# Dilated attention stage: weight, merge and staging transfers issued from ScalarE's queue, and half of a merge one step later

## The chip, the cores and the metric

One core of a Trainium2 chip. The metric is device time in microseconds (us) from start to end of one execution; lower is better. Engines: PE (TensorE), DVE (VectorE), ACT (ScalarE), POOL (GpSimd), and SP (SyncE), which only issues transfers (DMAs).

## What is computed

A bidirectional encoder of two layers on 1024 tokens of width 1024 in float32. Layer 0 mixes tokens by latent attention, layer 1 by dilated sliding-window attention; each layer ends with a squared-ReLU MLP. The change is in layer 1's mixer:

```python
DIL_GROUPS = ((128, 1), (512, 4), (2048, 16))     # (window, dilation)
def dilated_mixer(h, pos, w_in, g_q, g_k, rel_bias, w_o):
    proj = (h @ w_in).reshape(B, S, N_DIL_GROUPS, 3, DIL_HEADS, DIL_HEAD_DIM)
    for gi, (window, dilation) in enumerate(DIL_GROUPS):
        q = rms_norm(proj[:, :, gi, 0], g_q[gi])
        k = rms_norm(proj[:, :, gi, 1], g_k[gi])
        v = proj[:, :, gi, 2]
        o, lse = dilated_group(q, k, v, pos, table, window, dilation)
    wts = jax.nn.softmax(jnp.stack(lses, axis=0), axis=0)
    o = jnp.einsum('gbsh,gbshd->bshd', wts.astype(o_all.dtype), o_all)
    return o.reshape(B, S, DIL_HEADS * DIL_HEAD_DIM) @ w_o
```

So there are three groups of 16 heads of width 64, with a relative-position bias, and for every token the three groups' outputs are merged with weights from their softmax denominators.

## The kernel before

The stage is the method `dil()`. It runs over a list of steps: three groups, in each eight pairs of heads (`pr`), in each pair four steps (`tp`) of a quarter of the tokens. Between groups stands a step without projection (`None`), in which the normalized input is permuted for the next dilation (casts into `hTp`, L2097 and L2099). A step takes some 9 us.

One step works on three things at once. PE computes the scores of an earlier step (`pss`, L1869), the query and key projections of this step (`psproj`, L414 to L416, each product in three float32 pieces of a high and a low part), transposes of the queries and keys of the step before (`psq`, L1844), and the product of probabilities and values (`psav`, L1937 and L1938).

The chain of a step, off PE: DVE adds the bias tile `bt` and takes the maximum (`pd`, L1883), ACT negates it (`dnb`, L1887), exponentiates (L1889) and writes the high half of the probabilities (`ph`, L1923), POOL or DVE the low half (L1924). SP then issues a transposing DMA (`pT`, L1925), and psav reads pT. Alongside, ACT squares the projection (`dsq`, L1828), DVE sums it (`dms`, L1829), ACT takes a logarithm and an exponential (`drl`, `dry`, L112 and L113), DVE and POOL scale (`qn`, L1833 and L1835), PE transposes (psq), and ACT and DVE write the key tile in two parts (`kT`, L1848 and L1849), which the next step's pss reads.

The transfers of the stage, all from SP's queue:

- `wqkr`: the weights of the pair two steps ahead, four DMAs for each pair (`dil_weights`, L1551, called by `fetch`). ACT makes the high part (`wqkh`, L121), DVE the low one (`wqkl`, L122).
- `bt`: two bias tiles for each step (L1878). `vraw`: values (L1788 to L1804).
- `U`: the outputs of groups 1 and 2, written to memory (L1955, L1959). `um`: these outputs read back for the merge in group 3, four DMAs for each pair (L2041). `oTd`: merged and transposed outputs of pairs 0 to 5, written to memory (L2032).
- `pT`: the transposes (L1925), one for each step.

The merge is in group 3: `finish` (L1949) runs when a pair's attention is done. `factors` (L1982) turns the stored maxima and sums into weights with small operations (L1992 to L1998); `merge` multiplies and adds (L2007, L2009), five operations of 128x512 on DVE for each half of the tokens. Before, both halves follow at once; in the next step `emit` transposes them on PE and stores them (`oTd`).

The order on each engine is not the order of the code. A scheduler places the instructions of all engines, and each engine then runs its own list strictly in order. An instruction whose semaphore isn't there holds everything behind it on its engine. Each DMA of SP's queue, and of ACT's, takes one of eight completion lanes (DMAHW0 to DMAHW7) in turn, and waits for the DMA that had the lane before to land.

Of the kernel before, what the change touches and what calls it, by code (L numbers as in the profile page):

```python
# [41 lines left out]
class K:  # L42
# [1496 lines left out]
        v = dram.rearrange("(l r) d -> r l d", r=16)  # L1539
        return [(64 * i, 64, v[2 * t + i]) for i in range(2)]  # L1540

    def dil_weights(self, g, pr, alloc=None):


        w_in = self.a["dil_w_in"][0]
        raws = []
        for half in range(2):
            raw = (alloc or self.G)("wqkr", (P, 4, 256), F32)
            for k in range(2):
                c0 = (g * 3 + k) * 1024 + 2 * pr * 64  # L1550
                self.nc.sync.dma_start(out=raw[:, :, k * P : (k + 1) * P],  # L1551
                                       in_=w_in[half * 512 : (half + 1) * 512, c0 : c0 + P].rearrange("(d p) f -> p d f", p=P))
            raws.append(raw)

        def split():
            out = []
            for raw in raws:
                hi, lo = self.G("wqkh", (P, 4, 256)), self.G("wqkl", (P, 4, 256))
                self.split(hi, lo, raw)
                out.append((hi, lo))  # L1560
            return out

        return split
# [185 lines left out]
    def dil(self, at0, at1, tail, wqk, vd):  # L1749
# [194 lines left out]
                last(u, 0)  # L1944

        O = [[[None] * 4 for _ in range(2)] for _ in range(2)]
        merged = []

        def finish(u):  # L1949
            g, pr = u["g"], u["pr"]  # L1950
            U = u["U"]
            if g < 2:
                dst = Ud[pr, :, g, :]
                if g == 0:
                    nc.sync.dma_start(out=dst.rearrange("(t p) e -> p t e", p=P), in_=U)  # L1955
                else:
                    v = dst.rearrange("(l p r) e -> p r l e", r=4, p=P)
                    for l in range(2):
                        nc.sync.dma_start(out=v[:, :, l, :], in_=U[:, l::2, :])  # L1959
                if pr == 7:  # L1960
                    sv = stat[:, g].rearrange("p t k h -> p t (k h)")
                    if g == 0:
                        nc.sync.dma_start(out=Sd[g].rearrange("(t p) e -> p t e", p=P), in_=sv)
                    else:
                        v = Sd[g].rearrange("(l p r) e -> p r l e", r=4, p=P)
                        for l in range(2):
                            nc.sync.dma_start(out=v[:, :, l, :], in_=sv[:, l::2, :])
                return

            if pr == 0:  # L1970
                for k in range(2):
                    v = Sd[k].rearrange("(l t r) e -> r l t e", t=8, r=2)
                    for i in range(2):
                        nc.sync.dma_start(out=stat[64 * i : 64 * i + 64, k].rearrange("p t k h -> p t (k h)"), in_=v[i])
            if pr < 7:
                f = factors(pr, 0, 8)
                for hf in range(2):
                    merge(u, hf, f[:, :, 4 * hf : 4 * hf + 4])
                merged.append((u, u["at"], (0, 1)))
            else:  # L1980
                last(u, 1)

# [33 lines left out]
        def emit(u, ths):  # L2016

            pr = u["pr"]
            if pr == 6:
                for k in range(2):  # L2020
                    for th in range(2):
                        O[k][th][3] = self.G(f"oT{k}", (P, 2, 512))
            for th in ths:
                ps = PS("psot")
                for i in range(4):
                    nc.tensor.transpose(ps[:, i * P : (i + 1) * P], u["U"][:, 4 * th + i, :], self.ident)
                if pr >= 6:
                    self.split(O[0][th][3][:, pr - 6, :], O[1][th][3][:, pr - 6, :], ps)
                else:
                    s_ = self.G("oT", (P, 2, 512))  # L2030
                    self.split(s_[:, 0, :], s_[:, 1, :], ps)
                    nc.sync.dma_start(out=oTd[pr, th], in_=s_.bitcast(F32))  # L2032

        def um(u, hfs):

            u.setdefault("um", [])
            v = Ud[u["pr"]].rearrange("(l t r) k e -> r l t (k e)", t=8, r=2)
            for hf in hfs:
                x = self.G("um", (P, 4, 2, P), F32)
                for i in range(2):  # L2040
                    nc.sync.dma_start(out=x[64 * i : 64 * i + 64].rearrange("p t k e -> p t (k e)"), in_=v[i][:, 4 * hf : 4 * hf + 4, :])  # L2041
                u["um"].append(x)


# [8 lines left out]

        def fetch(n):
            if n in firsts:
                loads[n] = self.dil_weights(*firsts[n][1:3])

        def fetch_split(n):
            if n in firsts:
# [51 lines left out]
        for n, step in enumerate(steps):  # L2111
# [23 lines left out]
            for u_, t_, _ in scored:  # L2135
                if u_["g"] == 2:
                    if u_["pr"] < 7:
                        if t_ == 7:
                            um(u_, (0, 1))
                    elif t_ in (1, 5):  # L2140
                        um(u_, (t_ // 4,))
            if step is not None:
                ps = PS("psproj")
                project(h, w, ps, 0, 2 * tp)
# [204 lines left out]
```

## Time and profile before

| | us |
|---|---|
| median of three runs | 3288.84 (3288.83 to 3289.92) |
| the profiled execution | 3296.57 |
| span of its trace | 3294.7 |
| dilated stage in the trace | 1645 to 2620 |
| PE busy, whole span | 3150.8 (96%) |
| DVE, ACT, POOL busy, whole span | 2406.2, 1735.6, 878.1 |

PE is the engine that works nearly all of the time, so an idle microsecond of PE is the thing to look for. The page's strip of 40 slices shows PE at nine tenths nearly everywhere; the stage lies in slices 20 to 32, where its clock is at nine tenths too, with 0.70 and 0.83 in the windows of the two changes of group (1950 to 1990 and 2260 to 2300). The busy shares of the other engines are averages over stages with different limits, and don't say which of them PE waits for; the waits do. A wait is put down to the semaphore that came last.

### The profile page before, as it was taken

The page shows a single profiled execution, that of the slowest core. Times are in us where ns is not written, and L with a number is a line of the kernel's source. Part 1 is how long each engine was busy: PE and PEld are TensorE (multiplying, and loading weights), DVE is VectorE, ACT ScalarE, POOL GpSimd, SP SyncE. Part 2 cuts the span into 40 slices and gives each one's busy share as a digit, 9 for nine tenths or more (in the row PEclk, how much of TensorE's full clock was granted, in tenths as well). Part 3 has the DMA queues.
Part 4 walks back from the last instruction along what each step waited for, and adds up shares of the span by engine and source line. Part 5 has one row for each costly group of instructions (what it writes and reads, how often), then busy time and mean ns, then how long its engine had stood idle before and what let it go on. Part 6 is the DMA issues. An engine that isn't in the chain of part 4 may idle for free. (4 is left out here: it accounts for less than half of the span.)

```text
span 3294.7 us, 50852 instructions
## 1 busy us (share of the span) xinstructions
PE 3150.8 (96%) x18034; PEld 2660.6 (81%) x18034; DVE 2406.2 (73%) x4272; ACT 1735.6 (53%) x3507; POOL 878.1 (27%) x1197
## 2 busy tenths in 40 slices
PE   6989999999999999899999979998998999999999
PEld 6877677778888788778899979997988788888887
DVE  5677777757977866787667776777778678778566
ACT  5547787755544433542246665667555355444342
POOL 7455555520111000001134343444333001110010
PEclk9999999999999999999999989998999999999999
DMA  5352322152654788536558866777777735439554
GB/s 189 119 186 82 103 94 88 63 191 78 213 185 170 279 243 283 168 106 209 195 142 177 189 149 161 180 169 161 146 174 169 211 96 204 143 143 322 205 191 128
DMA packets 538990, 552.31 MB, mean 168 GB/s; under 512 B 199493, under 2 KB 421106, under 8 KB 538730
## 3 DMA queue, kind: packets, MB, share of 16 engines
q1 hardware_dynamic: 511370, 457.69, 49.2%
q0 software_dynamic: 27360, 91.31, 7.5%
q8 instruction: 144, 2.36, 0.3%
q14 instruction: 116, 0.95, 0.1%
HBM read 376.17 MB, written 132.62 MB: 154 GB/s over the span
## 5 line engine op out<-in xcount | busy, mean ns | idle before, releaser
L415 PE MATMUL psm<-dl,dh 128*128 128x512 f32 x896 | 351.1, 392 | 8.5 <-DVE dl L122 8.4
L414 PE MATMUL psm<-hf,wf 128*128 128x512 f32 x896 | 350.1, 391 | 2.6 <-ACT wf L121 2.6
L416 PE MATMUL psm<-dh,dl 128*128 128x512 f32 x896 | 350.1, 391 | 0.0
L415 PE MATMUL psm<-hf,wf 128*128 128x512 f32 x896 | 349.6, 390 | 0.0
L416 PE MATMUL psm<-hf,wf 128*128 128x512 f32 x896 | 346.9, 390 | 0.4 <-DVE wf L122 0.4
L414 PE MATMUL psm<-dh,dh 128*128 128x512 f32 x896 | 335.0, 391 | 4.8 <-ACT dh L121 4.8
L414 PE MATMUL psproj<-wqkh,hTp 128*128 128x256 f32 x1024 | 306.0, 299 | 0.0
L415 PE MATMUL psproj<-wqkl,hTp 128*128 128x256 f32 x1024 | 293.9, 287 | 0.0
L416 PE MATMUL psproj<-wqkh,hTp 128*128 128x256 f32 x1024 | 293.5, 287 | 0.0
L121 ACT ACTIVATE dh<-ufr 128x1024 fp32r<-128x1024 f32 x112 | 118.3, 1057 | 175.8 <-PE psm L416 51.0
L414 PEld LDWEIGHTS psproj<-wqkh,hTp 128*128 128x128 f32 x1024 | 200.5, 196 | 9.2 <-issue 1.6
L415 PEld LDWEIGHTS psm<-dl,dh 128*128 128x128 f32 x896 | 169.0, 189 | 46.3 <-DVE dl L122 11.6
L414 PEld LDWEIGHTS psm<-dh,dh 128*128 128x128 f32 x896 | 168.3, 188 | 42.1 <-ACT dh L121 7.3
L414 PEld LDWEIGHTS psm<-hf,wf 128*128 128x128 f32 x896 | 168.6, 188 | 40.2 <-ACT wf L121 5.5
L415 PEld LDWEIGHTS psproj<-wqkl,hTp 128*128 128x128 f32 x1024 | 200.7, 196 | 0.0
L416 PEld LDWEIGHTS psproj<-wqkh,hTp 128*128 128x128 f32 x1024 | 200.3, 196 | 0.0
L416 PEld LDWEIGHTS psm<-hf,wf 128*128 128x128 f32 x896 | 168.5, 188 | 36.1 <-DVE wf L122 1.2
L416 PEld LDWEIGHTS psm<-dh,dl 128*128 128x128 f32 x896 | 169.0, 189 | 35.2
L415 PEld LDWEIGHTS psm<-hf,wf 128*128 128x128 f32 x896 | 168.6, 188 | 34.6
L122 DVE TENSOR_TENSOR dl<-ufr,dh 128x1024 fp32r<-128x1024 f32 x112 | 136.8, 1222 | 78.1 <-ACT dh L121 59.5
L745 DVE TENSOR_REDUCE mx<-pmx 128x1 f32<-128x512 f32 x256 | 165.2, 682 | 28.2 <-PE pmx L743 27.9
L1924 POOL TENSOR_TENSOR ph<-pd,ph 128x512 f16<-128x512 f32 (+1 forms) x120 | 122.8, 1028 | 226.9 <-ACT ph L1923 211.4
(399 smaller groups left out, 8950.1 us busy)
## 6 DMA issues: line engine op xcount, KB each, us to landing
ufr<-uf SPq DMA_DIRECT2D x112, 512.0 KB
adaw<-in_ada_w SPq DMA_DIRECT2D x96, 512.0 KB
w2r<-in_mlp_w SPq DMA_DIRECT2D x96, 512.0 KB
w1r<-in_mlp_w SPq DMA_DIRECT2D x64, 512.0 KB
bt<-bias SPq DMA_DIRECT2D x128, 256.0 KB
wqkr<-in_dil_w_in SPq DMA_DIRECT2D x96, 256.0 KB
qkv<-st SPq DMA_DIRECT2D x32, 512.0 KB
hraw<-qkv SPq DMA_DIRECT2D x32, 512.0 KB
```

Of the source, the lines that this page charges most:

```text
L121: nc.scalar.activation(hi, src, AF.Copy)
L122: (lo_eng or nc.vector).tensor_tensor(lo, src, hi.bitcast(F32), op=ALU.subtract)
L414: mm(out, lh, rh, start=first, stop=False)
L415: mm(out, lh, rl, start=False, stop=False)
L416: mm(out, ll, rh, start=False, stop=last)
L745: nc.vector.tensor_reduce(maxes[h][:, 2 * j + b : 2 * j + b + 1], ps, op=ALU.max, axis=AX.X)
L1924: (nc.gpsimd if i or g == 2 else nc.vector).tensor_tensor(lo, p, hi, op=ALU.subtract)
```

## The change

Three kinds of transfer are issued by `nc.scalar` (ACT's queue) instead of `nc.sync` (SP's): `wqkr` as called by `fetch` (92 of 96; the first pair's four stay with SP), all 32 `um`, all 12 `oTd`: 136 DMAs. The sizes and the addresses are the same. In group 3, `finish` merges only the first half of the tokens, with factors for that half; the second half, with its own factors, is put on the list `merging` and done in the next step, ahead of the projections, and is emitted a step later than before. That adds six small DVE operations and one exponential for each of seven pairs.

```diff
-    def dil_weights(self, g, pr, alloc=None):
+    def dil_weights(self, g, pr, alloc=None, eng=None):
...
-                self.nc.sync.dma_start(out=raw[:, :, k * P : (k + 1) * P],
+                (eng or self.nc.sync).dma_start(out=raw[:, :, k * P : (k + 1) * P],
...
-        merged = []
+        merged, merging = [], []
...
             if pr < 7:
-                f = factors(pr, 0, 8)
-                for hf in range(2):
-                    merge(u, hf, f[:, :, 4 * hf : 4 * hf + 4])
-                merged.append((u, u["at"], (0, 1)))
+                merge(u, 0, factors(pr, 0, 4))
+                merged.append((u, u["at"], (0,)))
+                merging.append((u, 1))
             else:
                 last(u, 1)
...
-            if pr == 6:
+            if pr == 6 and 0 in ths:
...
-                    nc.sync.dma_start(out=oTd[pr, th], in_=s_.bitcast(F32))
+                    nc.scalar.dma_start(out=oTd[pr, th], in_=s_.bitcast(F32))
...
-                    nc.sync.dma_start(out=x[64 * i : 64 * i + 64].rearrange("p t k e -> p t (k e)"), in_=v[i][:, 4 * hf : 4 * hf + 4, :])
+                    nc.scalar.dma_start(out=x[64 * i : 64 * i + 64].rearrange("p t k e -> p t (k e)"), in_=v[i][:, 4 * hf : 4 * hf + 4, :])
...
-                loads[n] = self.dil_weights(*firsts[n][1:3])
+                loads[n] = self.dil_weights(*firsts[n][1:3], eng=nc.scalar)
...
+            if merging:
+                u_, hf = merging.pop(0)
+                merge(u_, hf, factors(u_["pr"], 4 * hf, 4))
+                merged.append((u_, n, (hf,)))
             if step is not None:
                 ps = PS("psproj")
                 project(h, w, ps, 0, 2 * tp)
```

Since the scheduler places all of it anew, the order changes in more places than these. Three of them follow. The numbers in the names tell buffers apart; what an instruction waits for stands in brackets.

**ACT in group 3, the step in which a pair's weights and `um` are loaded.** Before, from the step's squares (`dsq`) to `kT`:

```order
L1828 ACTIVATE dsq_31206<-psproj_31138 128x512 [waits PE_49,Pool_49]
L121 ACTIVATE wqkh_31359<-wqkr_31224 128x1024 [waits DMAHW1_49,DMAHW0_49,DVE_49]
L112 ACTIVATE drl_31211<-dms_31207,eps 128x8 [waits DVE_49]
L113 ACTIVATE dry_31210<-drl_31211 128x8 [waits Activation_49]
L1887 ACTIVATE dnb_31248<-stat,ln_20890 128x2 [waits DVE_49]
L1887 ACTIVATE dnb_31259<-stat,ln_20890 128x2 [waits DVE_49]
L1889 ACTIVATE pd_31245,stat<-pd_31245,dnb_31248 128x128 [waits Activation_49]
L1889 ACTIVATE pd_31245,stat<-pd_31245,dnb_31248 128x128
L1889 ACTIVATE pd_31256,stat<-pd_31256,dnb_31259 128x128 [waits Activation_49,Pool_49]
L1889 ACTIVATE pd_31256,stat<-pd_31256,dnb_31259 128x128
L1923 ACTIVATE ph_31241<-pd_31245 128x256 [waits DMAHW3_49,Activation_49]
L1848 ACTIVATE kT_30951<-psq_31297 128x2x256 [waits PE_49]
```

The changed kernel, the first part of the same step:

```order
L1828 ACTIVATE dsq_31217<-psproj_31140 128x512 [waits PE_49,Pool_49]
L121 ACTIVATE oT_31201<-psot_31196 128x512 [waits PE_49]
L1551 DMA wqkr_31232<-in_dil_w_in 128x4x128 [waits DMAHW7_49]
L1551 DMA wqkr_31232<-in_dil_w_in 128x4x128 [waits DMAHW1_49]
L112 ACTIVATE drl_31222<-dms_31218,eps 128x8 [waits DVE_49]
L1551 DMA wqkr_31235<-in_dil_w_in 128x4x128 [waits DMAHW2_49]
L113 ACTIVATE dry_31221<-drl_31222 128x8 [waits Activation_49]
L1551 DMA wqkr_31235<-in_dil_w_in 128x4x128 [waits DMAHW3_49]
L2031 DMA oTd<-oT_31201 128x1024 [waits DMAHW4_49,DVE_49]
L1887 ACTIVATE dnb_31259<-stat,ln_20890 128x2 [waits DVE_49]
```

and its second part:

```order
L2040 DMA um_31277<-U 64x4x256 [waits DMAHW6_49]
L1889 ACTIVATE pd_31256,stat<-pd_31256,dnb_31259 128x128 [waits Activation_49]
L1889 ACTIVATE pd_31256,stat<-pd_31256,dnb_31259 128x128
L1887 ACTIVATE dnb_31270<-stat,ln_20890 128x2 [waits DVE_49]
L2040 DMA um_31277<-U 64x4x256 [waits DMAHW0_49]
L1923 ACTIVATE ph_31252<-pd_31256 128x256 [waits Activation_49]
L1889 ACTIVATE pd_31267,stat<-pd_31267,dnb_31270 128x128 [waits Activation_49,Pool_49]
L1889 ACTIVATE pd_31267,stat<-pd_31267,dnb_31270 128x128
L2040 DMA um_31280<-U 64x4x256 [waits DMAHW1_49]
L2040 DMA um_31280<-U 64x4x256 [waits DMAHW2_49]
L1923 ACTIVATE ph_31252<-pd_31267 128x256 [waits Activation_49]
L1848 ACTIVATE kT_30946<-psq_31308 128x2x256 [waits PE_49]
```

Nine DMAs now stand among the step's activations. Four `um` lie between `dnb` and the second `ph`; the third and the fourth wait for the lanes of the second and third `wqkr` (DMAHW1 and DMAHW2). `kT` comes behind the second `ph`, where it stood ahead of it, and the split of the weights (`wqkh`) has left the place behind `dsq`.

**SP at the change from group 1 to group 2.** Before:

```order
L1925 DMA_TRANSPOSE pT_24870<-ph_24869 128x16x128 [waits DVE_49,DMAHW0_49,PE_49,Pool_49]
L1878 ISA
L1878 DMA bt_25218<-bias_135 128x2x256 [waits DMAHW5_49,DMAHW1_49,DVE_49]
L1878 ISA
L1878 DMA bt_25282<-bias_135 128x2x256 [waits DMAHW6_49,DMAHW2_49,DVE_49]
L1878 ISA
L1878 DMA bt_25293<-bias_135 128x2x256 [waits DMAHW7_49,DMAHW3_49,DVE_49]
L1878 ISA
L1878 DMA bt_25418<-bias_135 128x2x256 [waits DMAHW4_49,DMAHW1_49,DVE_49]
L1925 DMA_TRANSPOSE pT_25024<-ph_25023 128x16x128 [waits PE_49,Pool_49]
```

The changed kernel:

```order
L1925 DMA_TRANSPOSE pT_24870<-ph_24869 128x16x128 [waits DVE_49,DMAHW0_49,PE_49,Pool_49]
L1878 ISA
L1878 DMA bt_25218<-bias_135 128x2x256 [waits DMAHW4_49,DMAHW1_49,DVE_49]
L1878 ISA
L1878 DMA bt_25282<-bias_135 128x2x256 [waits DMAHW6_49,DMAHW2_49,DVE_49]
L1925 DMA_TRANSPOSE pT_25024<-ph_25023 128x16x128 [waits DVE_49,DMAHW5_49,PE_49,Pool_49]
L1878 ISA
L1878 DMA bt_25293<-bias_135 128x2x256 [waits DMAHW7_49,DVE_49]
L1878 ISA
L1878 DMA bt_25418<-bias_135 128x2x256 [waits DMAHW1_49,DVE_49]
```

Two bias loads that wait for DVE have moved behind the transpose `pT_25024`. On POOL, the low half `ph_25023` that it needs has moved ahead of two casts into `hTp`.

**SP at the change from group 2 to group 3.** Before:

```order
L1878 DMA bt_29893<-bias_136 128x2x256 [waits DMAHW5_49,DMAHW1_49,DVE_49]
L1925 DMA_TRANSPOSE pT_29608<-ph_29607 128x16x128 [waits DMAHW0_49,DVE_49,DMAHW6_49,PE_49,Pool_49]
L1959 DMA U<-U_28598 512x1x128 [waits DVE_49]
L1878 ISA
L1878 DMA bt_29905<-bias_136 128x2x256 [waits DMAHW2_49,DVE_49]
```

The changed kernel:

```order
L1878 DMA bt_29893<-bias_136 128x2x256 [waits DMAHW5_49,DMAHW1_49,DVE_49]
L1959 DMA U<-U_28598 512x1x128 [waits DVE_49]
L1925 DMA_TRANSPOSE pT_29608<-ph_29607 128x16x128 [waits DMAHW0_49,DMAHW7_49,PE_49,Pool_49]
L1878 ISA
L1878 DMA bt_29905<-bias_136 128x2x256 [waits DMAHW2_49,DVE_49]
```

The store of `U_28598`, which waits for DVE's reduction of `psav`, has moved ahead of the transpose.

## Prediction

> **What bounds the kernel now.** I read the page first, then the windows of the dilated stage, then what TensorE (PE) waits for there, by group, and last the timelines around the longest of those waits. A window row holds its length and the busy time of PE, PE's weight loads, DVE, ACT and POOL, then the granted clock, the DMA share and GB/s; the first is group 3 with its pair steps, the second the sum of six windows from 1645 to 2620 us. A wait row holds total us, times, longest.
>
> ```profile
> 2300.00:2560.00 260.00, 240.14 (x2105) 227.91 (x2104) 206.61 (x595) 145.86 (x499) 87.06 (x108) 0.96 0.73 163
> sum 975.00, PE 905.47 PEld 847.96 DVE 715.08 ACT 575.02 POOL 349.70; mean PE 150.91 PEld 141.33 DVE 119.18 ACT 95.84 POOL 58.28
> PE psav L1937 <- DMA pT<-ph: 40.4, 22, 11.3
> PE pss L1869 <- DVE kT L1849: 16.0, 14, 6.1
> ```
>
> The change touches only this stage, and there PE is busy for 905.5 of 975 us. So 69.5 us, 2.1% of the span, is all that any rearrangement could win, and 40.4 of them are spent in front of the probability products psav, until the transposed probabilities pT have landed. The second cause, 16.0, is the key tile kT in front of the scores pss. The same question for pT asked in the windows of group 1 (1645 to 1950), group 2 (1990 to 2259) and group 3 (2300 to 2560) gives these rows, the fourth being kT in group 3:
>
> ```profile
> PE psav L1937 <- DMA pT<-ph: 8.1, 8, 2.1
> ...
> PE psav L1937 <- DMA pT<-ph: 3.5, 5, 1.7
> ...
> PE psav L1937 <- DMA pT<-ph: 16.2, 6, 4.5
> PE pss L1869 <- DVE kT L1849: 1.9, 3, 0.8
> ```
>
> The rest of pT's 40.4, 12.6, lies at the two changes of group (1950 to 1990, 2259 to 2300). Whether SyncE's queue (SP) is to blame differs: SP's own waits say whom the transpose stood waiting for, in group 1 and in group 3.
>
> ```profile
> SPq L1925 <- DVE ph L1924: 32.1, 16, 4.1
> ...
> SPq L1925 <- POOL ph L1924: 43.7, 17, 5.0
> ```
>
> In group 1 DVE's ph alone held 16 of the transposes (others waited for POOL): SP was free before the data was there, so taking work off SP helps little. In group 3 it is 17 of about 30 (one in each step of some 9 us); the others found SP occupied or had been delayed otherwise. One pair's turn shows how:
>
> ```profile
> 2347.25 1.43 SPq L1551 DMA_DIRECT2D wqkr<-in_dil_w_in  x2
> ...
> 2349.45 1.70 SPq L1551 DMA_DIRECT2D wqkr<-in_dil_w_in  x2
> ...
> 2352.24 3.40 SPq L2041 DMA_DIRECT2D um<-U  x4
> ...
> 2357.28 3.40 SPq L1925 DMA_TRANSPOSE pT<-ph  x1
> ...
> 2352.83 0.67 POOL L1924 TENSOR_TENSOR ph<-pd,ph 128x256 f16<-128x256 f32 x1
> ...
> 2364.31 0.34 PE L1937 MATMUL psav<-vs,pT 128*128 128x192 bf16 x1 [4.32 <-DMA pT<-ph]
> ```
>
> ph was complete at 2353.50, the transpose was issued at 2357.28, 3.8 us late, because two weight loads and four um loads went first; it then took 7.0 us to land, and PE stood 4.32 us.
>
> **The change, part by part.** What moves is issue time. The three rows give min, median and maximum in ns on SP.
>
> ```profile
> L1551 SPq DMA_DIRECT2D wqkr<-in_dil_w_in x96: 368/536/1582, 1614.8 to 2498.2; - x96
> ...
> L2041 SPq DMA_DIRECT2D um<-U x32: 579/615/1419, 2313.6 to 2568.3; - x32
> ...
> L2032 SPq DMA_DIRECT2D oTd<-oT x12: 502/590/1180, 2346.6 to 2533.1; - x12
> ```
>
> 92 x 0.536 + 32 x 0.615 + 12 x 0.590 = 49.3 + 19.7 + 7.1 = 76 us leave SP. No DMA issued by ACT is in this trace, so its price there is unknown: at the one end nothing (it hides behind the running activation), at the other SP's own time. I take SP's time, the nearest row, and keep both ends. In groups 1 and 2 this is 4 x 0.536 = 2.1 us per pair of heads, in a stage with these ACT waits:
>
> ```profile
> ACT drl L112 <- DVE dms L1829: 108.4, 73, 6.2
> ACT dnb L1887 <- DVE stat L1883: 79.4, 79, 6.1
> ACT wqkh L121 <- DMA wqkr<-in_dil_w_in: 68.7, 25, 15.2
> ```
>
> The order puts the four loads around drl and ahead of dnb; waits of 1.5 us at the one and 1.0 at the other cover most of 2.1, so I cost it at nothing; without that cover it would be 2.1 for 16 pairs at most, some of it in front of pT. The transposes there no longer share SP's queue with loads. Of 8.1 + 3.5 = 11.6 us I take **-3** for groups 1 and 2, a quarter, since SP mostly stood ready anyway; bounds -8 and +5.
>
> By the Trainium skill ("DMA: Bandwidth & Descriptors", section "Queues, rings and completion order") SP and ACT each own one ring on each of the same 16 DMA engines, so that a transpose need no longer stand behind the weights' packets in one ring. This trace has one issuing engine only for these transfers and can't show it; by that rule alone the 7.0 us to landing would shrink, and the term would tend to its -8.
>
> First change of group:
>
> ```profile
> 1944.17 15.77 SPq L1878 DMA_DIRECT2D bt<-bias  x4
> 1960.06 2.82 SPq L1925 DMA_TRANSPOSE pT<-ph  x1
> ...
> 1952.33 1.55 POOL L2099 TENSOR_SCALAR hTp<-hsl 128x512 fp32r<-128x512 f32 x1
> 1953.83 1.57 POOL L1924 TENSOR_TENSOR ph<-pd,ph 128x512 f16<-128x512 f32 x1
> ...
> 1960.88 0.70 DVE L1849 TENSOR_TENSOR kT<-psq,kT 128x512 fp32r<-128x512 f32 x1
> ...
> 1965.19 0.34 PE L1937 MATMUL psav<-vs,pT 128*128 128x192 bf16 x1 [11.30 <-DMA pT<-ph]
> ...
> 1967.44 1.65 PE L1869 MATMUL pss<-kT 64*128 64x256 f32 x12
> ```
>
> Two bias loads stood for a buffer of DVE in front of this transpose; the new order has it ahead of them, and POOL's ph ahead of two casts of that length, so ph is done near 1955.4 - 3.1 = 1952.3. With the same 5.1 us from issue to use, psav starts near 1957.4 and ends 2.2 later, but kT is finished only at 1961.6. So pss comes at 1961.6 instead of 1967.4: 5.8 at best, of which I take **-5** (bounds -7.7, if kT also moves, and -3): kT is what is late next.
>
> Second change of group, where the order is worse:
>
> ```profile
> 2258.59 1.92 SPq L1925 DMA_TRANSPOSE pT<-ph  x1
> 2263.61 0.57 SPq L1959 DMA_DIRECT2D U<-U  x1
> ...
> 2262.56 1.02 DVE L1939 TENSOR_REDUCE U<-psav 128x128 f32<-128x384 f32 x2
> ...
> 2262.88 0.34 PE L1937 MATMUL psav<-vs,pT 128*128 128x192 bf16 x1 [1.16 <-DMA pT<-ph]
> ...
> 2267.07 1.22 PE L1869 MATMUL pss<-kT 64*128 64x256 f32 x8 [1.15 <-DVE kT L1849]
> ```
>
> The U store now precedes the transpose, and it waits for DVE's reduction, which ends at 2263.6 behind a row of casts. The transpose goes from 2258.6 to 2264.2, psav 5.6 later; the 1.15 that pss waits for kT, and about 1 us of a like wait after it, are absorbed: **+3.5** (bounds +2 and +5.6).
>
> Group 3. The SP delay goes: of 16.2 I count 14 won; a little is left, since the transposes still land behind other traffic. The price is on ACT. In the step that used to follow, four um loads now stand between dnb, the exponentials and ph, and kT comes behind all of them and behind the second ph:
>
> ```profile
> 2350.41 0.57 ACT L1848 ACTIVATE kT<-psq 128x512 fp32r<-128x512 f32 x1
> ...
> 2350.89 0.41 ACT L1923 ACTIVATE ph<-pd 128x256 f16<-128x256 f32 x1
> ...
> 2351.02 0.69 DVE L1849 TENSOR_TENSOR kT<-psq,kT 128x512 fp32r<-128x512 f32 x1 [1.08 <-ACT kT L1848]
> ...
> 2352.63 0.98 PE L1869 MATMUL pss<-kT 64*128 64x256 f32 x12
> ```
>
> In a step without loads kT is complete at 2351.71 and pss starts at 2352.63: 0.92 us of slack. 4 x 0.615 + 0.41 = 2.87 us of delay makes pss 1.95 late. Some pairs have more slack, and an issue may overlap the activation before it, so I take 1.5 for each of seven pairs: +10.5. The four wqkr and the oTd issue ahead of dnb are covered by its wait. Group 3: -14 + 10.5 = **-3.5** (bounds -14 with a free issue, +13 with full price and loads that hold ACT).
>
> The split merge:
>
> ```profile
> L2009 DVE TENSOR_TENSOR U<-U,um x32: 677/690/1059, 2331.1 to 2602.9; 128x512 f32<-128x512 f32 x32
> ```
>
> Half a merge is five such operations, near 0.69 us each, 3.4 us, done one step later; a second set of small factor operations is new, six on DVE and one exponential for each of seven pairs. DVE is idle 53 us of group 3's 260 and the results have a step in hand: 0 (bounds -2, as the burst on DVE halves, and +10, seven times some 1.5 us, if DVE became the bound).
>
> **Sum:** -3 - 5 + 3.5 - 3.5 + 0 = -8 us. The profiled execution took 3296.57 us, 7.7 above the median of the runs, 3288.84; it would take 3288.6, and the median becomes **3281 us**.
>
> **Rivals.**
> *The issue is free on ACT.* Then kT isn't late and group 3 gives -14, groups 1 and 2 up to -4: -20, 3269 us. For it: an activation of 0.4 to 1 us usually runs as the next instruction is issued. Against it: no issue of these on SP took less than 0.368 us.
> *The transposes land no sooner.* What held pT was the traffic, not the queue: 7.0 us to landing with a share of 0.73 of all DMA engines' time in group 3. Then groups 1 and 2 give 0, group 3 loses by kT what the earlier issue wins, and the changes of group leave -1.5: near 3288 us. By the Trainium skill ("DMA: Bandwidth & Descriptors", section "Issuing engines are not separate DMA queues") transfers from all issuers run on the same 16 engines and spreading them saves issue time only; the share of 0.73 agrees that they are well used.
> *ACT is held at the um loads: slower.* The third and fourth um wait, before issue, for the second and third wqkr of that pair to land (eight completion lanes are used in turn by both queues). Between those loads and them stand two wqkr, an oTd and two um (2.9 us of issues), the mean waits of drl and dnb (2.5), and some small activations: 6 us or a little more. The second two loads above were issued from 2349.45, and what they feed,
>
> ```profile
> 2358.78 1.06 ACT L121 ACTIVATE wqkh<-wqkr 128x1024 fp32r<-128x1024 f32 x1 [4.38 <-DMA wqkr<-in_dil_w_in]
> ```
>
> started 9.3 us later, as they landed. Landing beyond 6 us decides it: every us goes into ph and kT. At 8.2 us it is 2.2 more per pair: pss 4.15 late, 29 for seven pairs against 14 won, in all -3 - 5 + 3.5 + 15 = +10.5, near 3299 us.
>
> **How the numbers follow.** A difference of 0.2% (6.6 us) is about what a measurement of this kernel tells from no change. Forecast 0.42, of which 0.33 below -6.6 and 0.09 within; free issue 0.13, faster; no sooner landing 0.20, 0.17 within and 0.03 slower; ACT held 0.25, 0.23 slower and 0.02 within. Faster 0.46, same 0.28, slower 0.26. All low bounds together would be -30, all high ones +31; they won't meet, and 8 times in 10 I expect 3266 to 3302: the free issue and a little beyond, and ACT held with its price.
>
> **What would show it.** Right: psav's wait for pT in group 3 down from 16.2 to under 4, pss's wait for kT up from 1.9 there to about 10, the 11.30 at 1965 below 6, and a psav wait near 2263 grown from 1.16 to about 6. ACT's issues of um near 0.6 us would confirm the price; near 0.1, the free issue. Wrong would be pT waits as large as now with SP idle (same traffic), or ACT idle at um for wqkr.

## The result and the profile after

The changed kernel takes 3311.83 us (median of six runs, 3307.61 to 3315.67), against 3288.84 for the kernel before on the same chip (six runs, 3280.49 to 3290.78). The ratio is 1.0074, with a 95% interval of 1.0063 to 1.0085: slower by 0.7%, where 0.24% faster was forecast. The profiled execution took 3309.74 us, 13.2 more than the profiled one before, and its span grew from 3294.7 to 3307.7.

The medians differ by 23.0 us, the two profiled executions by 13.2: that of the kernel before took 7.7 us more than its median, that of the changed kernel 2.1 less. So what follows explains some 13 of the 23. The rest fits the granted clock. It is 0.982 and 0.983 in the two profiled executions, but 0.979 to 0.981 in the other five of the changed kernel, and 0.983 on average (0.980 to 0.987) in the 74 executions of the kernel before that ran beside the experiments below. By an estimate from these, 0.003 of PE's 3150 us are 9 us. In the trace a long stall is followed by a lower clock: in the changed kernel PE stood 3.97 us for pT until 1944.65; the granted clock was 0.99 from 1944 to 1945 and 0.50 from 1945.2 to 1948.2, and a product of psav (L1937) took 0.37 us there instead of 0.25.

The first view is the table of the dilated stage by windows. Columns: length, busy time of PE, PE's weight loads, DVE, ACT and POOL, granted clock, DMA share, GB/s. The windows are group 1, first change of group, group 2, second change, group 3 and its end, cut so that each holds the same long waits. The cuts fall only roughly at the same places of the program (group 1 holds 2463 products after and 2570 before), but PE works without a pause in the 10 us by which that cut differs. Before (the row of group 3 and the sum stand in the prediction):

```profile
1645.00:1950.00 305.00, 291.99 (x2570) 274.79 (x2569) 213.21 (x560) 183.71 (x514) 114.20 (x141) 1.00 0.72 166
1950.00:1990.00 40.00, 23.40 (x171) 21.53 (x172) 28.12 (x59) 23.84 (x55) 18.01 (x19) 0.70 0.58 145
1990.00:2260.00 270.00, 256.98 (x2396) 244.93 (x2395) 197.87 (x548) 178.79 (x523) 112.12 (x166) 0.99 0.74 168
2260.00:2300.00 40.00, 35.97 (x292) 33.01 (x289) 32.78 (x87) 26.51 (x75) 15.54 (x20) 0.83 0.84 175
...
2560.00:2620.00 60.00, 57.00 (x299) 45.79 (x299) 36.51 (x88) 16.30 (x49) 2.78 (x4) 0.97 0.70 192
```

and after:

```profile
1645.00:1945.00 300.00, 281.65 (x2463) 265.86 (x2462) 203.06 (x537) 171.90 (x486) 106.39 (x133) 0.99 0.74 165
1945.00:1990.00 45.00, 36.01 (x288) 32.22 (x285) 40.65 (x84) 35.78 (x84) 29.13 (x26) 0.81 0.64 150
1990.00:2255.00 265.00, 254.92 (x2384) 243.98 (x2383) 197.47 (x551) 179.03 (x524) 109.64 (x168) 0.99 0.77 172
2255.00:2300.00 45.00, 37.00 (x332) 34.70 (x332) 32.58 (x87) 27.48 (x80) 15.82 (x19) 0.88 0.76 167
2300.00:2575.00 275.00, 240.05 (x2072) 227.10 (x2069) 211.38 (x655) 146.87 (x502) 86.49 (x109) 0.95 0.65 152
2575.00:2635.00 60.00, 57.49 (x294) 46.58 (x294) 29.51 (x67) 14.89 (x45) 0.00 (x1) 0.96 0.69 203
sum 990.00, PE 907.12 PEld 850.44 DVE 714.65 ACT 575.94 POOL 347.48; mean PE 151.19 PEld 141.74 DVE 119.11 ACT 95.99 POOL 57.91
```

Length less PE's busy time is PE's idle time. It is 13.0, 16.6, 13.0, 4.0, 19.9 and 3.0 us before (69.5) and 18.3, 9.0, 10.1, 8.0, 35.0 and 2.5 after (82.9). PE's work is the same within 1.7 us, so the 13.4 us of idle time account for the 13.0 by which the span grew. So there is one large loss, group 3 with 15.1; a loss in group 1 of 5.3; a gain at the first change of 7.6 and in group 2 of 2.9; and a loss at the second change of 4.0.

What PE waits for over the whole stage after the change, the first rows:

```profile
PE pss L1869 <- DVE kT L1849: 33.1, 22, 4.8
PE psav L1937 <- DMA pT<-ph: 27.1, 15, 6.5
```

The two causes have changed places: pT was 40.4 and is 27.1, kT was 16.0 and is 33.1. In group 3 (2300 to 2575) the rows are:

```profile
PE pss L1869 <- DVE kT L1849: 17.6, 11, 4.0
PE psq L1844 <- DVE qn L1833: 4.4, 3, 2.4
PE psy L414 <- DVE qn L1833: 4.1, 1, 4.1
PE psq L1844 <- POOL qn L1835: 4.1, 4, 2.4
```

There is no wait for pT any more; 16.2 us of it are gone. In its place stand kT, up from 1.9 to 17.6 (with 3.6 more for ACT's part of it), and waits put down to the scaled queries and keys, qn, up from 1.4 to 12.6. (The single wait of 4.1 stands in front of the output projection psy, which doesn't read qn; there qn is only the DVE operation that had just ended.) DVE makes most of these. What DVE itself waited for in that window, first before (2300 to 2560) and then after:

```profile
DVE kT L1849 <- ACT kT L1848: 12.9, 14, 2.1
```

```profile
DVE um L2006 <- DMA um<-U: 22.3, 7, 6.1
```

Before, DVE often stood ready in front of kT and no row of its waits names `um`. After, it stands 22.3 us in front of a merge multiplication until `um` has landed. The longest of these, in the timelines of ACT, DVE and PE (first the start, then the duration; the wait in brackets):

```profile
2308.87 0.73 ACTq L2040 DMA_DIRECT2D um<-U  x1
...
2310.02 0.58 ACTq L2040 DMA_DIRECT2D um<-U  x1
2310.05 0.47 ACT L1887 ACTIVATE dnb<-stat,ln 128x2 f32<-128x2 f32 x2
...
2310.99 0.58 ACTq L2040 DMA_DIRECT2D um<-U  x1
...
2311.71 0.58 ACTq L2040 DMA_DIRECT2D um<-U  x1
...
2312.58 0.57 ACT L1848 ACTIVATE kT<-psq 128x512 fp32r<-128x512 f32 x1
...
2310.78 0.69 DVE L1833 TENSOR_TENSOR qn<-psproj,dry 128x512 f32<-128x512 f32 x1
2317.52 1.29 DVE L2006 TENSOR_TENSOR um<-um,mgf 128x512 f32<-128x512 f32 x2 [6.05 <-DMA um<-U]
2318.73 0.68 DVE L1849 TENSOR_TENSOR kT<-psq,kT 128x512 fp32r<-128x512 f32 x1
...
2319.47 0.86 PE L1869 MATMUL pss<-kT 64*128 64x256 f32 x10 [4.05 <-DVE kT L1849]
```

ACT's part of kT was complete at 2313.15. DVE's part could have followed at once. But in DVE's list two multiplications of the merge stand ahead of it, `um` was only issued between 2308.9 and 2312.3, and DVE stood until 2317.5. PE stood 4.05 us. The code adds no such order; the scheduler made it. Before, the factors (L1992 to L1998) needed the statistics of both halves, so the multiplications came after kT. (The first of a pair ran at 2328.22 there, behind a kT at 2325.99.) Now the first half's factors need the first half's statistics alone, are ready earlier, and the multiplications with `um` are placed earlier, ahead of kT. (That is read from the dependences; f1 below, with joint factors, has no such wait.)

The changes of group went as the forecast said. PE's waits there, after:

```profile
1963.06 0.34 PE L1937 MATMUL psav<-vs,pT 128*128 128x192 bf16 x1 [0.96 <-DMA pT<-ph]
...
1967.98 1.22 PE L1869 MATMUL pss<-kT 64*128 64x256 f32 x8 [1.88 <-DVE kT L1849]
...
2262.33 0.34 PE L1937 MATMUL psav<-vs,pT 128*128 128x192 bf16 x1 [6.53 <-DMA pT<-ph]
```

The 11.30 is 0.96, and kT is late next: two thirds of the pss behind this psav wait 1.88 for it, where the pss behind the 11.30 waited for nothing. (Ahead of the psav, pss waits for kT in both kernels, 3.77 before and 3.55 after.) At the second change 1.16 became 6.53.

Group 1 lost where a small gain was expected. Its wait for pT, after (8.1 in 8 times before):

```profile
PE psav L1937 <- DMA pT<-ph: 14.5, 8, 4.0
```

The step with the weights' loads, before (SP's timeline) and after (SP, ACT and PE):

```profile
1707.99 3.57 SPq L1925 DMA_TRANSPOSE pT<-ph  x1
1711.62 1.67 SPq L1551 DMA_DIRECT2D wqkr<-in_dil_w_in  x3
```

```profile
1704.98 5.15 SPq L1925 DMA_TRANSPOSE pT<-ph  x1
...
1704.43 0.94 ACTq L1551 DMA_DIRECT2D wqkr<-in_dil_w_in  x2
...
1706.18 0.38 ACTq L1551 DMA_DIRECT2D wqkr<-in_dil_w_in  x1
1706.63 1.46 ACTq L1551 DMA_DIRECT2D wqkr<-in_dil_w_in  x1
...
1715.76 0.26 PE L1937 MATMUL psav<-vs,pT 128*128 128x192 bf16 x1 [3.52 <-DMA pT<-ph]
```

Before, three of the four loads stood behind the transpose in SP's queue. After, all four (256 KB each) are issued by ACT in the 3.7 us from 1704.4, around the transpose's issue at 1704.98, and PE uses pT 10.8 us after its issue, having waited 3.52. This holds for six of the first 22 transposes of group 1, one in each pair: by the completion events in the trace they landed 8.3 to 10.7 us after issue, and 4.3 to 6.1 in the same steps before. What the loads delayed there were other transposes (worst 8.4).

Last, ACT's issue of `um`, min, median and maximum in ns:

```profile
L2040 ACTq DMA_DIRECT2D um<-U x32: 581/587/1324, 2308.9 to 2584.5; - x32
```

An issue is as long on ACT as on SP (615 there). But it lies beside the activation ahead of it: in the step shown, from the first dnb at 2310.05 to kT at 2312.58 are 2.53 us with three `um` issued beside them; in the kernel before, the pair's turn shown in the prediction had 2.26 from dnb at 2348.15 to kT at 2350.41.

### The profile page after: what moved, and what is told of

Same layout as the page of the kernel before. It is cut to its first block, busy times and chain, and to the rows that moved or that the text cites. A ratio compares the mean times of both kernels' runs of the same rounds, so it can differ in the third digit from the quotient of the medians.

```text
span 3307.7 us, 50890 instructions
## 1 busy us (share of the span) xinstructions
PE 3147.8 (95%) x18034; PEld 2660.0 (80%) x18034; DVE 2405.6 (73%) x4314; ACT 1737.3 (53%) x3514; POOL 876.5 (26%) x1197
## 5 line engine op out<-in xcount | busy, mean ns | idle before, releaser
L415 PEld LDWEIGHTS psm<-dl,dh 128*128 128x128 f32 x896 | 169.4, 189 | 45.9 <-DVE dl L122 10.8
L122 POOL TENSOR_TENSOR pl<-p,ph 128x1024 fp32r<-128x1024 f32 x58 | 141.2, 2435 | 136.1 <-ACT ph L121 125.8
```

The source lines that it names most:

```text
L122: (lo_eng or nc.vector).tensor_tensor(lo, src, hi.bitcast(F32), op=ALU.subtract)
L415: mm(out, lh, rl, start=False, stop=False)
```

## The experiments

All ratios are against the kernel before on the same chip, with 95% intervals. Theories are told apart by group 3's rows of kT and by the time:

- **ACT's queue** (the forecast's own price): issues on ACT make ACT's part of kT late.
- **The wait for `um`** (A2 in the expectations): the split places a multiplication that waits for `um` on DVE, and this wait is the loss.
- **The place in DVE's order** (A3 in the expectations): the loss is whatever of the merge, waiting or not, stands ahead of a kT that has no slack.
- And for group 1: **transfers beside the transpose**, or the issue time on ACT.

### The parts one at a time: e1, e2, e3, e4

e1 is the changed kernel with `um` back on SP:

```diff
-                    nc.scalar.dma_start(out=x[64 * i : 64 * i + 64]...
+                    nc.sync.dma_start(out=x[64 * i : 64 * i + 64]...
```

> The changed kernel with um back on SP's queue; wqkr and oTd stay on ACT, the merge stays split. Theory A (late merge data: the split puts the first multiplications of a half merge ahead of kT on DVE, and um, issued by ACT some 5 us later in the step than by SP, hasn't landed: DVE stood 22.3 us in 7 waits): DVE's wait for um falls from 22.3 to under 10 us, PE's waits for kT and qn in group 3 from 34 to about 20 us, time about 3302 us. Theory B (ACT's issue time of um delays ph and kT): kT comes earlier by 2.4 us a pair, time also near 3300, but DVE's wait for um stays above 15.

Measured: 3321.27 us, ratio 1.0083 (1.0069 to 1.0097). Both theories had expected about 3300; the time rose instead. The kT row in group 3 grew to 28.0 in 7 waits, with DVE's wait for `um` at 18.1. Taking the four issues of `um` from ACT didn't help, so these issues are not what makes kT late.

e2 is the changed kernel with all transfers on ACT, but both halves merged at once, as before:

```diff
-                merge(u, 0, factors(pr, 0, 4))
-                merged.append((u, u["at"], (0,)))
-                merging.append((u, 1))
+                f = factors(pr, 0, 8)
+                for hf in range(2):
+                    merge(u, hf, f[:, :, 4 * hf : 4 * hf + 4])
+                merged.append((u, u["at"], (0, 1)))
```

> The changed kernel with the merge of both halves at once, as before; all three kinds of transfer stay on ACT. Theory A: the multiplications stand later on DVE, no wait for um is left (under 3 us from 22.3), group 3 loses nothing and keeps the absence of transpose waits: 15 to 20 us faster than the changed kernel, near 3295 us. Theory B: the um issues still stand in front of kT on ACT: no gain, 3308 to 3315 us.

Measured: 3291.54, ratio 1.0004 (0.9990 to 1.0017). The whole loss is gone. PE's waits in group 3:

```profile
PE pss L1869 <- ACT kT L1848: 5.0, 3, 2.8
PE pss L1869 <- DVE qn L1833: 4.9, 1, 4.9
PE pss L1869 <- DVE kT L1849: 3.8, 8, 0.9
```

DVE has no wait for `um`. kT, ACT's and DVE's part together, is 8.8.

e3 is the kernel before with only `wqkr` on ACT (the lines of the diff on `dil_weights` and `fetch`).

> The kernel before with only the wqkr loads on ACT. Theory C (in group 1 the transposes of a pair's first step land later because the weight loads of ACT's queue share the DMA engines with them, where they stood behind the transposes in SP's queue): PE's wait for pT in group 1 is again near 14 us instead of 8, the first change of group gains about 9, group 3 loses nothing: 3280 to 3288 us. Rival D (group 1's loss is ACT's issue time in front of ph): the transposes land as quickly as before, in 4 to 6 us, but are issued later.

Measured: 3291.76, ratio 1.0000 (0.9990 to 1.0010), without the expected gain in time. Group 1's wait for pT is 13.4, as in the changed kernel; group 3 has kT 3.7 and ACT's kT 4.9, together 8.6. So `um` and `oTd` on ACT (e2 less e3) add 0.2 to kT, and nothing to the time that these runs can tell.

e4 is the kernel before with only the split of the merge, all transfers on SP.

> The kernel before with only the split merge, all transfers on SP. Theory A with both causes needed: DVE waits for um less than 8 us, time within 5 us of before (3284 to 3294). If the split alone does it: DVE waits for um 15 us or more and the time is 3297 to 3305 us.

Measured: 3305.92, ratio 1.0040 (1.0025 to 1.0055), some 13 us (8 to 18) for the split alone. DVE's wait for `um` lies between the two expectations, the time just above the second. PE's and DVE's rows in group 3:

```profile
PE pss L1869 <- DVE kT L1849: 17.8, 8, 4.4
PE pss L1869 <- ACT kT L1848: 8.7, 4, 3.4
```

```profile
DVE um L2006 <- DMA um<-U: 12.8, 5, 4.0
```

That is nearly the 17.6 of the changed kernel, with no transfer on ACT's queue. The wait for pT in group 3 is down to 0.5 here too, though no transfer was moved. Two things go with it and aren't separated: PE, held by kT, comes to pT later; and in this order no transpose of group 3 is issued more than 0.4 us after the ph that it needs (before, the latest were 3.8, 2.8 and 1.7 us behind). The first change of group keeps its 11.3.

### What in the split costs: f1, f2, h2

f1 is the changed kernel with one set of factors for both halves; only the second half's multiplications come a step later.

```diff
-                merge(u, 0, factors(pr, 0, 4))
+                f = factors(pr, 0, 8)
+                merge(u, 0, f[:, :, 0:4])
...
-                merging.append((u, 1))
+                merging.append((u, 1, f[:, :, 4:8]))
```

> The changed kernel (all three transfers on ACT, second half merged one step later) with the factors of both halves computed at once, as before; only the second half's multiplications come a step later. Theory A2 (the split's harm is that factors of half the tokens are ready a step early, so the order puts the um multiplications in front of kT before um has landed): the multiplications fall back behind kT, DVE's wait for um is under 3 us instead of 22.3, time as without the split, 3288 to 3294 us. Theory B2 (what harms is merging and emitting the second half a step later): still 3300 us or more.

Measured: 3306.49, ratio 1.0062 (1.0049 to 1.0074). DVE's wait for `um` is gone, and the loss is not:

```profile
PE pss L1869 <- DVE kT L1849: 15.1, 6, 7.2
```

Two of these waits are of 6.81 and 7.16. Ahead of the first, ACT's part of kT was done at 2407.9; DVE, at work without a pause on the merge, the scaling and the split of the weights, came to its own at 2415.05. The wait alone was not the cause.

f2 is the changed kernel with `um` loaded one step earlier (`if t_ == 5:` for `if t_ == 7:`).

> The changed kernel with um loaded one step earlier; the split, its factors and its place on DVE stay. Theory A2: um has landed when DVE comes to it, the wait is under 3 us, group 3's loss goes, 3287 to 3295 us. Theory B2, or a price of the split's own operations in front of kT (1.3 us a pair and more): DVE's wait for um is gone all the same, but PE still waits 25 us or more in group 3 and the time stays at 3300 or above.

Measured: 3284.56, ratio 0.9999 (0.9990 to 1.0009). The loss is gone, but not as expected: under 3 us of the wait were to be left, and the rows of PE and DVE are

```profile
PE pss L1869 <- DVE kT L1849: 7.9, 8, 2.4
```

```profile
DVE um L2006 <- DMA um<-U: 18.8, 7, 4.1
```

DVE waits nearly as long as before the edit (18.8 against 22.3), but in another step of the pair, where kT has more room. For the kT that followed each of these seven waits PE stood 4.5 us in all; in the changed kernel it was 16.1. The longest in f2, 4.08, cost PE 1.26; in the changed kernel a wait of 6.05 cost it 4.05, and one of 3.86 cost it 3.56.

h2 is the changed kernel with both halves merged together, one step later; no multiplication then meets a missing `um`.

```diff
-                merge(u, 0, factors(pr, 0, 4))
-                merged.append((u, u["at"], (0,)))
-                merging.append((u, 1))
+                merging.append((u, (0, 1)))
```

> The changed kernel (all three transfers on ACT), with both halves merged one step later, factors at once. Theory A3 (group 3's price is whatever DVE has in front of kT in a step: a wait for um or merge operations; here five and more merge operations stand ahead of kT in the order, and um has long landed): no wait for um on DVE, but PE waits 15 us or more for kT in group 3, 3298 to 3312 us. Theory A2 (only the wait for um costs): PE waits under 8 us for kT in group 3, 3286 to 3294 us.

Measured: 3308.17, ratio 1.0070 (1.0055 to 1.0084); no DVE wait for `um`, and kT 17.5 in 13 waits, the longest 6.2. There, DVE, ACT and PE (the merge has lines 2004 and 2006 in this kernel):

```profile
2405.75 3.30 DVE L2004 TENSOR_TENSOR um<-um,mgf 128x512 f32<-128x512 f32 x3
2408.97 1.64 DVE L2006 TENSOR_TENSOR U<-U,um 128x512 f32<-128x512 f32 x1
2410.53 1.21 DVE L122 TENSOR_TENSOR wqkl<-wqkr,wqkh 128x1024 fp32r<-128x1024 f32 x1
2411.67 0.68 DVE L1849 TENSOR_TENSOR kT<-psq,kT 128x512 fp32r<-128x512 f32 x1
...
2404.43 0.57 ACT L1848 ACTIVATE kT<-psq 128x512 fp32r<-128x512 f32 x1
...
2412.40 1.43 PE L1869 MATMUL pss<-kT 64*128 64x256 f32 x10 [6.17 <-DVE kT L1849]
```

ACT's part of kT was done at 2405.0. DVE, busy without a pause, came to its own at 2411.67. A3 holds and A2 falls: what counts is what stands ahead of kT in DVE's list, waiting or working. (In f1 and h2 the split of the weights, wqkl, stands there as well.) The other suspects fall too. The split's additional small operations aren't it, since f1 and h2 don't have them; nor is it the later second half (B2 in the expectations), since f2 has that and no loss.

Nor is it a chance of one order. All five versions with the second half later and `um` loaded where it was (the changed kernel, e1, e4, f1, h2) are 0.40 to 0.83% slower than the kernel before. The three with both halves at once (e2, e3, f4) and the two with `um` early (f2, h3) lie between -0.13 and +0.04%.

### The loads beside the transposes: f4, h3, g1, h1, h5

f4 is e3 with the loads of group 1 left on SP:

```diff
+                loads[n] = self.dil_weights(*firsts[n][1:3], eng=nc.scalar if firsts[n][1] else None)
```

> The kernel before with wqkr on ACT for the pairs of groups 2 and 3 only. Theory C (group 1 loses because ACT's weight loads run beside the transposes; the first change of group gains by the order of SP's queue): PE's wait for pT in group 1 is back at 8 us, the change of group keeps its gain of about 9, the second change loses 3: 3281 to 3286 us, ratio 0.997 to 0.9985. If the gain at the change of group hangs on group 1's own loads, nothing is gained: ratio 1.000.

Measured: 3280.87, ratio 0.9987 (0.9978 to 0.9996): the only version faster than the kernel before, and by little (0.997 to 0.9985 was expected). Group 1's wait for pT:

```profile
PE psav L1937 <- DMA pT<-ph: 9.7, 5, 4.1
```

against 13.4 in e3. The six transposes with loads beside them landed 8.5 to 10.0 us after issue in e3; here, with these loads back on SP, the same six took 4.3 to 6.1. The 11.3 at the first change is 1.5 here, though the loads of that group stayed on SP. h1 and h5 below, which move no load at all, have 2.5 and 3.0 there; g1 keeps 11.1. So this gain belongs to the order that falls out at that place, which several edits change.

h3 joins f2 and f4, which should have added their gains.

> The changed kernel with um loaded one step earlier, and wqkr on ACT only for the pairs of groups 2 and 3. Theories A3 and C together: group 3 as in the run with um early (no loss), group 1 without the longer transposes, the first change of group keeps its gain: 3276 to 3282 us, ratio 0.9965 to 0.9985 against the kernel before. If group 1's loss comes from elsewhere: ratio 1.000.

Measured: 3286.23, ratio 0.9994 (0.9983 to 1.0005). A miss: group 1 kept its 9.7, but the order in group 3 came out otherwise again, with kT 11.9 (f2 had 7.9) and 3.8 for qn.

The last three ask why the transposes of group 1 land late. g1 adds to the kernel before four tiny unread loads for each pair, issued by ACT in group 1.

> The kernel before, and in group 1 for each pair four further loads of 4 KB each from ACT, whose data nobody reads (additional work, at the place where the changed kernel issues wqkr). Theory C (the bytes beside the transposes do the harm): transposes of a pair's first step still land in 4 to 6 us, PE's wait for pT in group 1 stays at 8 us, time within 3 us of before. Theory D (ACT's issue time in front of ph): PE waits 13 us or more for pT in group 1, 5 us slower.

Measured: 3295.86, ratio 1.0033 (1.0021 to 1.0045), which answers another question. The scheduler put all 28 loads into the first 22 us of the stage, so they stood beside no transposes (pT 8.2 in group 1). Yet the time rose by 10.8 us; the trace shows a new 6.0 us wait of pss for qn in group 3, far from any edit. (h1 and h5 have the same wait; they gain at the first change of group, where g1 doesn't.)

So h1 and h5 tie the extra transfers to a step: ACT writes `dsq` to memory four times, in the second step of each pair of group 1, 256 KB each in h1, 4 KB each in h5 (`0:8` for `0:512`). Their programs are the same but for this number.

```diff
+            if g == 0 and tp == 1:
+                for d in range(4):
+                    nc.scalar.dma_start(out=dumd[d][:, 0:512], in_=sq[:, 0:512])
```

> The kernel before, and in group 1, in the second step of each pair, ACT issues behind dsq four transfers of 256 KB of dsq to memory, which nobody reads (additional work: the bytes and the place of the moved wqkr, which themselves stay on SP). Theory C (bytes of ACT's queue share the DMA engines with the transposes): transposes of that step land in 8 to 11 us instead of 4 to 6, PE waits 13 us or more for pT in group 1. Theory D (the issue time): as the next run.

> The same kernel as the run before it, instruction for instruction, but each of the four transfers moves 4 KB instead of 256. Theory C: transposes land as in the kernel before, 4 to 6 us, PE waits 7 to 10 us for pT in group 1. Theory D (ACT's issue time, 2 us in front of drl, makes ph late): PE waits as long as with the full transfers, 13 us or more.

Measured: h1 3296.74, ratio 1.0028 (1.0018 to 1.0039); h5 3287.43, ratio 1.0008 (0.9997 to 1.0019). Group 1's wait for pT in h1 and in h5:

```profile
PE psav L1941 <- DMA pT<-ph: 14.9, 7, 4.1
```

```profile
PE psav L1941 <- DMA pT<-ph: 9.8, 7, 2.8
```

The issue time, the same in both, isn't group 1's loss; the bytes beside are worth 5.1 us of these waits. (The times differ by 9.3; h1's profiled execution also had the lower granted clock, 0.979 against 0.983.) How the bytes act is only half as expected. The seven transposes of h1 with the writes beside them landed 5.5 to 9.5 us after issue, those of h5 4.6 to 7.9: three of h1's reached 8 us, against all six in the changed kernel. The one of 9.5 (7.1 in h5) cost PE 3.52, against 1.32 in h5. But the two largest waits, 3.98 and 4.07 (2.81 and 2.29 in h5), came of the transposes after these: SP issued them 2.0 and 2.9 us late, behind bias loads (0.9 and 0.5 in h5), and they then landed in 4.5 to 4.7.

## Why the prediction was wrong, step by step

| term | predicted, us | PE's idle time, after less before |
|---|---|---|
| groups 1 and 2 | -3 (-8 to +5) | +5.3 - 2.9 = +2.4 |
| first change of group | -5 (-7.7 to -3) | -7.6 |
| second change | +3.5 (+2 to +5.6) | +4.0 |
| group 3 and the split | -3.5 and 0 | +15.1 |
| last stretch | none | -0.5 |
| sum | -8 | +13.4 |

**The step that failed is the split merge, "0 (bounds -2 ... and +10 ...)".** Its reason was that DVE is idle 53 us of group 3's 260 and the results have a step in hand. Both are averages: they say that the work fits, not where it lands in DVE's list. The prediction had itself found that kT has 0.92 us of slack, and used it against ACT alone. The same 0.92 stands against DVE: two multiplications of 0.68 us ahead of kT are over it, and with a wait for `um` of up to 6.05 it is far over. e4 measures the split alone at 0.40%, or 13 us (8 to 18), around the upper bound of 10. With the transfers on ACT it costs more: 1.0074 for the changed kernel against 1.0004 for e2, which differ in the split alone, are 0.70% or some 23 us. e2 also shows that without the split nothing of the loss is left; f1, f2 and h2 show that the place ahead of kT is the cause, and not the wait as such. The order that would have told it could have been read beforehand: in DVE's list of the changed kernel, multiplications with `um` stand between qn and kT, and `um` is issued by ACT in the same step.

**Group 3's pT stalls went as said, and it wasn't worth 14.** All 16.2 went in the changed kernel, but e4, with all transfers on SP, has them down to 0.5 as well. And late issue on SP was less of their cause than the step took it for ("the others found SP occupied or had been delayed otherwise"): of the 28 transposes from 2300 to 2560 in the kernel before, three were issued more than 1 us after their ph, 8.3 us in all, and the six that PE waited for took 5.7 to 9.2 us to land. The clean case is e2: pT 1.1, and still no gain, since the rest of group 3's waits, 3.3 before (kT 1.9, qn 1.4), are 17.8 (kT 8.8, qn 4.9 and 4.1). PE runs close behind three chains at once, pT, kT and qn; with the first one early, it stands for the others.

**The price on ACT: the mechanism was there, its size and its source were off.** Predicted was kT late by 10.5, for four `um` issues. e2, which has all of these issues and not the split, has kT late by 8.8, 6.9 more than before. But e3 has 8.6 with no `um` on ACT. Those of `um` and `oTd` together add 0.2: their length was as forecast (0.587), but they lie beside activations, so the length was no sign of a price. What delays kT comes with `wqkr`: f4 has 8.0 too, while g1, h1 and h5, with `wqkr` on SP and both halves merged at once, have 1.9 to 2.8. Whether it is their issue, their landing or the new order isn't shown. The sign named beforehand, "kT up from 1.9 to about 10", came in at 17.6 and seemed to confirm this term. It was the other one: a sign that two causes share confirms neither. The other three signs of being right (pT in group 3 under 4, the 11.30 below 6, about 6 near 2263) came true as well, with the time going the other way: none of them looks at the split.

**The changes of group: right**, the first larger than taken (7.6, within its bound of 7.7), the second 4.0 for 3.5. The 11.30 went to 0.96, and kT is late next, as was said.

**Groups 1 and 2: wrong in group 1.** The step said that the transposes "no longer share SP's queue with loads" and counted this as a gain. The trace shows the other side: with the loads in the transpose's own queue it landed in 4.3 to 6.1 us, with the loads issued beside it from the other queue in 8.3 to 10.7. By the Trainium skill ("DMA: Bandwidth & Descriptors", section "Queues, rings and completion order") each DMA engine takes turns, packet by packet, between the rings that have work, and SP and ACT each own a ring on every one of them; the weights then take turns with the transpose, where they stood behind it. The landing times in the changed kernel agree with that (8.3 to 10.7 us for the six transposes with weights beside). e3 and f4 show that the place of the loads does it (8.5 to 10.0 with them on ACT, 4.3 to 6.1 with them on SP). That it is by taking turns isn't shown: h1, with as many bytes beside, has such landing times for three of seven transposes only.

**The rivals.** "The transposes land no sooner" is nearest for the transfers alone: e2 and e3 at 1.0004 (0.9990 to 1.0017) and 1.0000 say that the move is worth nothing that can be measured, and not the 0.24% forecast, as the gains and losses of the stretches cancel. "ACT is held at the um loads", the forecast's slower case, didn't happen: ACT's waits in group 3 that end with a landing of `wqkr` come to one of 1.2 us. It is DVE that is held at `um`. "Issue is free on ACT" is nearly right for `um` and didn't matter. The slower side came true through a mechanism that none of the rivals had. The measured median lies 9.8 us over the range's upper end, since that end took the split at 0 and not at its own upper bound.

**What stays open.** Orders that differ for reasons far from an edit move the time by some 10 us (g1: +0.33% with nothing but tiny loads at the stage's start; h3's kT against f2's). Differences below about 0.3% between these versions are therefore not put down to one mechanism without a row of the trace, f4's gain of 0.13% among them. And h1 leaves open how bytes beside a transpose act: of its 5.1 us, 2.2 came with a transpose that landed later, and some 3 with bias loads that held the next transposes on SP. Why the clock is lower in the slower versions is seen only as far as it falls after single stalls.

## What to carry to other kernels

A free engine on average says nothing about one instruction: for work that is put on an engine with a fixed order, find the operation with the least slack on that engine (here kT with 0.92 us), and see in the new order what now stands ahead of it and what that waits for. Moving transfers to a second queue frees the first one's issue time, but it also takes away the order between them, and what was behind a critical transfer may then run beside it. When a predicted sign appears, undo the cause alone before believing it: here kT was late as forecast, and for another reason.

## What the hardware showed that was not expected

- A DMA issue on ACT's queue takes as long as on SP's (0.587 and 0.615 us for `um`) but lies beside a running activation: three issues made the stretch from dnb to kT 0.27 us longer (2.53 against 2.26).
- A transpose of one step's probabilities in group 1 with 1 MB of weight loads issued at the same time from the other queue landed 8.3 to 10.7 us after issue, and 4.3 to 6.1 in the same steps of the kernel before, with all of it in one queue. With the loads moved alone (e3) it was 8.5 to 10.0, and with those of group 1 back on SP (f4) 4.3 to 6.1.
- A stall of PE costs more than its length: after one of 3.97 us in the changed kernel the granted clock was 0.50 for the next 3 us, and psav's products there took 0.37 instead of 0.25 us.
